# Layer 1 of a four-layer trunk: rotary scores from split operands, and the second rotary queries moved ahead of the heads

## Chip, cores and metric

The kernel runs on one core of one Trainium2 chip. The metric is the device time of one execution in microseconds, given as the median of several runs. A profiled execution of the same program gives the trace: what each engine (PE = TensorE, with PEld for its weight loads; ACT = ScalarE; DVE = VectorE; POOL = GpSimd; SP = SyncE, which issues the loads) did at which microsecond of its span.

## What is computed

The trunk has two layers here (DEPTH = 2): block-sparse attention and a gated MLP, then multi-head latent attention and a second gated MLP, on 256 tokens of width 2048. The change touches only the latent attention of layer 1. Cut to what matters:

```python
def mla_attention(h, pos, wq_a, g_qa, wq_b, wkv_a, g_kva, wkv_b, g_qn, g_kn, g_qr, g_kr, wo):
    cq = rms_norm(h @ wq_a, g_qa)                          # 256 x 512
    q = (cq @ wq_b).reshape(B, S, H, NOPE + RD)            # 16 heads, 128 + 64
    q_nope = rms_norm(q[..., :NOPE], g_qn)
    q_rope = rope(rms_norm(q[..., NOPE:], g_qr), pos, RD)  # 64 rotary features a head
    kv_a = h @ wkv_a                                       # 256 x (512 + 64)
    ckv = rms_norm(kv_a[..., :MLA_KV_RANK], g_kva)
    k_rope = rope(rms_norm(kv_a[..., MLA_KV_RANK:], g_kr)[:, :, None, :], pos, RD)[:, :, 0]
    kv = (ckv @ wkv_b).reshape(B, S, H, NOPE + VD)
    k_nope = rms_norm(kv[..., :NOPE], g_kn)
    v = kv[..., NOPE:]
    ...
        s = (jnp.einsum('bqhd,bkhd->bhqk', qn, k_nope)
             + jnp.einsum('bqhr,bkr->bhqk', qr, k_rope)).astype(F32) * scale
```

The last term is the rotary score: every head has 64 rotary query features of its own, and all heads share one rotary key of 64 features.

## The kernel before, in words

**Weights and split products.** All weight matrices are streamed from HBM in the order of their use, as 370 units of up to 1 MB (L138 to L155), each cut into 2 to 4 pieces of 128 rows by 512 or 288 columns. `Stream.split` (L92) makes of each piece a high part on ACT (L104) and a low remainder on DVE (L105), both in type fp32r. A product of two split operands is three products: high times high, low times high, high times low. With tokens as output rows (`tok_major`, L227) one piece is six products of 512 (or 288) columns at L235; with features as output rows (`feat_major`, L251) it is twelve products of 256 columns at L261 to L263. Operands that are not split are plain f32; for those one product in the program is two products in the trace. The score products (L473, L476) and the value products (L520, L521) are of this kind.

**The order of work** is written out by hand. Every piece is a quantum; `add` (L222) appends it, and `at(q, f)` (L216) hangs a piece of side work behind quantum q. The loop at L984 walks the quanta: first `ws.split` (L987), which has split all pieces up to the third one behind the current one, then the products, then the side work in the order in which it was hung. Each engine executes its own instructions strictly in this order, so a side step that waits on ACT or DVE also holds the splits that stand behind it on that engine, and PE has three further pieces whose parts are ready.

**Layer 1 attention** (L753 to L971) runs in this order of quanta: the query latents (L869); the first half of the rotary queries, heads 0 to 7, four pieces (`rotary_queries(0, 2)`, L920); the key latents and rotary key, 2 x 16 pieces of 288 columns (L922); group 0 of four heads, with queries, keys and values in four pieces each (L948); then the second half of the rotary queries, heads 8 to 15 (L950); groups 1 to 3; then the output projection. The side work that matters:

- `rotary_queries` (L895): evacuation to `qr`, squares (L379), `hr` by a power on POOL (L392), scaling on ACT (L413), rotation on DVE (L435 to L440), and 28 and 29 quanta behind its last piece the two pairs of turns (L449): four 128 x 128 transposes into a PSUM tile `tp` (a pool of two), then one ACT copy (L457) to `qrT`. `qrT` holds two heads in one slot, 64 partitions each.
- The key side: `kva_stats` (L774), with `kvr` on POOL; `kva_scale` (L793); `kva_rotate` (L799), which writes the rotary key twice side by side; `kva_turn` (L813), four transposes of the latents with their evacuation to `ckvT` (L821, L822); `kr_turn` (L826). The last two make two f32 tiles `kr[0]` and `kr[1]` in `room`: POOL writes zeros to all 128 rows (L833), and DVE copies the key to the upper or lower 64 (L834). A head's rotary score multiplies a slot of two heads with the tile that is zero on the other head's rows.
- `Head.plan` (L530): scores and mask, exponentials, normalisation, three transposes (L509), the copy `pT` (L514), values (L520), and the parts of the output (L527, L528).

`DVE` also makes the squares of every query and key head, so it is shared by splits, norms, rotations and softmax.

Of the kernel before, what the change touches and what calls it, by code (L numbers as in the profile page):

```python
# [10 lines left out]
F32 = mybir.dt.float32  # L11
# [6 lines left out]
P = 128  # L18
# [97 lines left out]
def trunk(ctx: ExitStack, tc: tile.TileContext, a, out):  # L116
# [29 lines left out]
    units += grouped("mla_wqr", 1, 0)  # L146
    units += units_of("mla_wkv_a", KVN)
    for g in range(4):
        if g == 1:
            units += grouped("mla_wqr", 1, 1)  # L150
        for name in ("mla_wkn", "mla_wqn", "mla_wv") if g else ("mla_wqn", "mla_wkn", "mla_wv"):
            units += grouped(name, 1, g)
# [200 lines left out]
    class Heads:  # L353
# [63 lines left out]
        def rotate(self, t, stages=(0, 1)):  # L417
# [11 lines left out]
            def part(name):  # L429
                r = att_pool.tile([P, 16 * 32], F32, name=name, bufs=2)  # L430
                return r[:, : n * rot].rearrange("p (n r) -> p n r", n=n)
# [31 lines left out]
    class Head:  # L463
# [4 lines left out]
        def scores(self):  # L468
            sc = ps_sc.tile([P, 512], F32, name="sc")
            qT, kT, i = self.qT(), self.kT(), self.i  # L470
            for q0, n, c in ((0, P, 0), (P, S, P)):
                o = sc[:, c : c + n]
                mm(o, qT[:, i, q0 : q0 + P], kT[:, i, :n], start=True, stop=self.rope is None)  # L473
                if self.rope is not None:
                    qr, kr = self.rope()
                    mm(o, qr[:, q0 : q0 + P], kr[:, :n], start=False, stop=True)  # L476
            self.sc = sc
# [34 lines left out]
        def turned(self):  # L512
            self.pT = att_pool.tile([P, 3 * P], F32, name="pT", bufs=2)
            nc.scalar.copy(self.pT, self.tp[:, : 3 * P])  # L514
# [241 lines left out]
    def open_mla():  # L756
# [6 lines left out]
        env["oT"] = att_pool.tile([P, H, 2 * S], F32R, name="oT", bufs=1)  # L763
        env["qrT"] = att_pool.tile([P, 8, S], F32, name="qrT", bufs=1)

# [8 lines left out]
    def kva_stats():  # L774
        ss = small.tile([P, NT, 2], F32, name="kvss")
        for t in range(NT):
            for k, (lo, hi) in enumerate(((0, 512), (512, 576))):
                junk = att_pool.tile([P, 512], F32, name="kvjunk", tag="ro1", bufs=2)
                nc.vector.tensor_tensor_reduce(
                    out=junk[:, : hi - lo], in0=env["ckv"][:, t, lo:hi], in1=env["ckv"][:, t, lo:hi],  # L780
                    scale=1.0 / (hi - lo), scalar=0.0, op0=ALU.mult, op1=ALU.add,
                    accum_out=ss[:, t, k : k + 1],
                )
# [42 lines left out]
    def kr_turn():  # L826
        tp = ps_tp.tile([P, 512], F32, name="tp")
        for t in range(NT):
            nc.tensor.transpose(
                tp[:, t * P : (t + 1) * P], env["krr"][:, t].rearrange("p i d -> p (i d)"), ident  # L830
            )
        for i in range(2):
            nc.gpsimd.memset(env["kr"][i], 0.0)  # L833
            nc.vector.tensor_copy(env["kr"][i][i * 64 : (i + 1) * 64, :], tp[i * 64 : (i + 1) * 64, :S])  # L834

# [57 lines left out]
    at(q_start + 20, gained_tables)  # L893

    def rotary_queries(u, step):  # L895
        state = {}
# [17 lines left out]
        for i0 in (0, 2):  # L914
            pair = {}
            at(q + step * 14 + i0 // 2, lambda p=pair, i0=i0: hs.turned(None, p, i0))
            at(q + step * 14 + i0 // 2, lambda p=pair, i0=i0: hs.turned_out(
                env["qrT"][:, 4 * u : 4 * u + 4], p, i0))

# [8 lines left out]
    def open_room():  # L928
        t = keep.tile([P, KD * 2 * S + 64], F32, name="room", tag="h")
        env["room"] = t[:, : 32 * S].rearrange("p (k s) -> p k s", k=32)  # L930
        env["kr"] = [env["room"][:, 28 + i] for i in range(2)]

# [4 lines left out]
    for r in range(4):  # L937
        at(q + 3 + r // 2, kva_turn, r)
    at(q + 9, kr_turn)

# [7 lines left out]
    for g in range(4):  # L948
        if g == 1:
            rotary_queries(1, 2)  # L950
        for kind in "kqv" if g else "qkv":
# [12 lines left out]
        for i in range(4):  # L964
            hd = Head(
                4 * g + i, lambda g=g: env["qT", g], lambda g=g: env["kT", g], lambda g=g: env["v", g],
                i, lambda: env["oT"], MLA_SCALE,
                rope=lambda h=4 * g + i: (env["qrT"][:, h // 2, :], env["kr"][h % 2]),
            )
# [133 lines left out]
```

## Time and profile before

| | |
|---|---|
| median of 3 runs | 2100.27 us (2099.58 to 2100.78) |
| profiled execution, its own time | 2100.51 us |
| its span, first to last instruction | 2098.7 us |
| mean granted TensorE clock | 1.000 |
| busy: PE / PEld / DVE / ACT / POOL | 2090.2 / 2014.8 / 1389.4 / 1134.2 / 45.6 us |
| rotary score products (L476) | 64 in the trace, 1199.8 to 1307.5 us |
| rotary queries, first turn (L449) and first wait behind the key latents | 1163.13 us, 1172.18 us |

A row of the timeline gives start, duration, engine, line, operation, output and inputs, partitions and columns, and the count of merged instructions; in brackets stands the idle time ahead of it and what ended it. Products overlap: a 512-column product shows a duration of 0.39 us while the next starts 0.23 us behind it. The pace, start to start, is what a product costs in a stream; the duration is what somebody waits who needs its result. Idle times in brackets count from the modelled end of the last product, so the loss against the pace is larger by the overlap. On ACT and DVE the next instruction likewise starts about 0.1 us ahead of the end of the last.

### The profile page before, as it was taken

What the parts mean: (1) busy time and instruction counts of PE and PEld (TensorE: products, weight loads), DVE (VectorE), ACT (ScalarE), POOL (GpSimd) and SP (SyncE); (2) the same over time, 40 slices, a digit from 0 to 9 for tenths busy, and PEclk for the clock granted to TensorE, in tenths of its full rate; (3) what the DMA queues carried; (4) which work ended last, traced back from release to release, by engine and by line L of the source; (5) the groups of instructions that cost most, each with busy time, mean ns of one, the idle gap of its engine ahead of it and who ended that gap; (6) DMA issues with size and microseconds to landing.
All of it is one profiled execution on the core that took longest, in us unless ns stands there. A gap on an engine that the chain in (4) does not pass through costs nothing.

```text
span 2098.7 us, 42064 instructions
## 1 busy us (share of the span) xinstructions
PE 2090.2 (100%) x16684; PEld 2014.8 (96%) x16684; DVE 1389.4 (66%) x3036; ACT 1134.2 (54%) x2206; POOL 45.6 (2%) x37
## 2 busy tenths in 40 slices
PE   9999999999999999999999999999999999999999
PEld 7888889999999999999999889999999999999999
DVE  6776666766666766655556786767766667655554
ACT  6555555655555555545455675655555555544443
POOL 0000000000000000000000110000000000000000
PEclk9999999999999999999999999999999999999999
DMA  7444445555555555555554533545555555555553
GB/s 272 161 166 176 168 170 188 190 191 201 190 193 201 187 196 199 192 195 195 195 192 158 176 139 106 196 181 200 186 197 198 187 199 195 189 205 208 194 206 131
DMA packets 59381, 391.81 MB, mean 187 GB/s; under 512 B 6960, under 2 KB 10032, under 8 KB 13232
## 3 DMA queue, kind: packets, MB, share of 16 engines
q1 hardware_dynamic: 59040, 388.87, 52.3%
q8 instruction: 130, 2.13, 0.4%
q14 instruction: 67, 0.55, 0.1%
q10 hardware_dynamic: 144, 0.26, 0.1%
HBM read 387.01 MB, written 2.10 MB: 185 GB/s over the span
## 4 chain that ended last, share of the span: by engine, by line
PE 97%; DVE 1%; DMA 1%; issue 0%; ACT 0%; POOL 0%; SPq 0%; ACTq 0%; POOLq 0%
PE acc L261 26%; PE acc L263 26%; PE acc L262 26%; PE acc L235 15%; PE sc L473 1%; PE tp L449 1%; DMA raw<-in_moba_wq 1%; PE sc L520 1%; PE tp L509 0%; PE sc L476 0%; PE sc L521 0%; DVE wlo L105 0%; DMA xT<-in_xT 0%; DVE junk L379 0%; POOL hr L392 0%
## 5 line engine op out<-in xcount | busy, mean ns | idle before, releaser
L105 DVE TENSOR_TENSOR wlo<-raw,whi 128x512 fp32r<-128x512 f32 (+1 forms) x1480 | 1000.5, 684 | 424.6 <-ACT whi L104 422.5
L104 ACT CAST whi<-raw 128x512 fp32r<-128x512 f32 (+1 forms) x1479 | 871.8, 614 | 461.4 <-PE acc L262 213.6
L261 PE MATMUL acc<-h,whi 128*128 128x256 f32 x2880 | 795.3, 276 | 0.0
L263 PE MATMUL acc<-h,wlo 128*128 128x256 f32 x2880 | 794.9, 276 | 0.0
L262 PE MATMUL acc<-h,whi 128*128 128x256 f32 x2880 | 794.9, 276 | 0.0
L262 PEld LDWEIGHTS acc<-h,whi 128*128 128x128 f32 x2880 | 540.7, 188 | 0.0
L261 PEld LDWEIGHTS acc<-h,whi 128*128 128x128 f32 x2880 | 540.6, 188 | 0.0
L263 PEld LDWEIGHTS acc<-h,wlo 128*128 128x128 f32 x2880 | 540.6, 188 | 0.0
L261 PE MATMUL acc<-a,whi 128*128 128x256 f32 x1408 | 388.6, 276 | 0.0
L262 PE MATMUL acc<-a,whi 128*128 128x256 f32 x1408 | 388.6, 276 | 0.0
L263 PE MATMUL acc<-a,wlo 128*128 128x256 f32 x1408 | 388.6, 276 | 0.0
L235 PE MATMUL acc<-whi,h 128*128 128x512 f32 (+1 forms) x896 | 279.8, 385 | 0.7 <-ACT whi L104 0.5
L261 PEld LDWEIGHTS acc<-a,whi 128*128 128x128 f32 x1408 | 264.3, 188 | 0.0
L262 PEld LDWEIGHTS acc<-a,whi 128*128 128x128 f32 x1408 | 264.3, 188 | 0.0
L263 PEld LDWEIGHTS acc<-a,wlo 128*128 128x128 f32 x1408 | 264.3, 188 | 0.0
L235 PEld LDWEIGHTS acc<-whi,h 128*128 128x128 f32 x896 | 164.7, 188 | 31.5 <-ACT h L279 1.3
L235 PE MATMUL acc<-wlo,h 128*128 128x512 f32 (+1 forms) x448 | 169.3, 378 | 0.3 <-DVE wlo L105 0.2
L261 PE MATMUL acc<-oT,whi 128*128 128x256 f32 x512 | 144.8, 283 | 0.0
L263 PE MATMUL acc<-oT,wlo 128*128 128x256 f32 x512 | 141.7, 277 | 0.0
L262 PE MATMUL acc<-oT,whi 128*128 128x256 f32 x512 | 141.6, 277 | 0.0
L675 DVE TENSOR_TENSOR g<-acc,rstd_b 128x256 f32<-128x256 f32 x88 | 37.5, 426 | 126.0 <-PE acc L263 123.1
L682 ACT ACTIVATE c<-g,par 128x256 f32<-128x256 f32 x88 | 53.1, 603 | 108.1 <-DVE g L675 108.1
(141 smaller groups left out, 1558.0 us busy)
## 6 DMA issues: line engine op xcount, KB each, us to landing
raw<-in_ffn_gu SPq DMA_DIRECT2D x176, 1024.0 KB, 4.8
raw<-in_ffn_down SPq DMA_DIRECT2D x88, 1024.0 KB, 4.8
raw<-in_moba_wk SPq DMA_DIRECT2D x16, 1024.0 KB, 4.8
raw<-in_moba_wv SPq DMA_DIRECT2D x16, 1024.0 KB, 4.8
raw<-in_moba_wo SPq DMA_DIRECT2D x16, 1024.0 KB, 4.8
raw<-in_mla_wo SPq DMA_DIRECT2D x16, 1024.0 KB, 4.8
raw<-in_moba_wq SPq DMA_DIRECT2D x13, 1024.0 KB, 4.8
raw<-in_mla_wkv_a SPq DMA_DIRECT2D x8, 576.0 KB, 3.7
```

The costliest lines, as they stand in the source:

```text
L104: self.nc.scalar.copy(hi[:, :n], w)
L105: self.nc.vector.tensor_tensor(lo[:, :n], w, hi[:, :n].bitcast(F32), op=ALU.subtract)
L235: mm(state["acc"][t][:, :n], src[:, kt, c : c + P], (t_lo if part == 1 else t_hi)[:, :n], start=kt == 0 and part == 0, stop=kt == k_last a ...
L261: mm(o, w_hi, src[:, kt, :S], start=first and k == 0, stop=False, skip_group_check=True)
L262: mm(o, w_hi, src[:, kt, S:], start=False, stop=False, skip_group_check=True)
L263: mm(o, w_lo, src[:, kt, :S], start=False, stop=kt == k_last, skip_group_check=True)
L449: nc.tensor.transpose(tp[:, (i * NT + t) * P : (i * NT + t + 1) * P], flat[:, t, c : c + P], ident)
L473: mm(o, qT[:, i, q0 : q0 + P], kT[:, i, :n], start=True, stop=self.rope is None)
L520: mm(o[:, :S], v[:, 0, vs], self.pT[:, :S], start=True, stop=False)
L675: nc.vector.tensor_tensor(self.g[:, 2:], self.gate["acc"][:, :S], self.norm.rstd_b, op=ALU.mult)
L682: nc.scalar.activation(self.c, self.g[:, 2:], AF.Identity, bias=par[:, cb : cb + 1], scale=self.cw(2))
```

## The change

1. **Rotary scores in parts.** The rotary key is kept once, as a high and a low part: `kr` is [128, 2, 256] in fp32r. `kr_turn` fills both with one ACT copy and one DVE subtraction over 128 rows (the key stands on both halves of the rows), in place of two POOL memsets and two DVE copies. Each head gets a slot of its own in `qrT`: the high part of its rotary queries on 64 rows, the low part on the other 64. One product of such a slot with the key's high part gives high times high plus low times high; a second one with the key's low part gives the rest. So a rotary score is two fp32r products for each of the two query blocks, in place of one f32 product.
2. **`rotary_out`** replaces the ACT copy of each pair of turns. For each half of the rows: an ACT copy of 64 rows x 512 to the slots (high), a DVE subtraction to the tile `qrlo` (low; one buffer), and a DMA on POOL's queue that carries the low part to the other 64 rows of the slots, 128 KB each. There are two pairs in each of the two rotary steps, so 8 copies, 8 subtractions and 8 DMAs in all, for 4 copies before.
3. **Order.** The second rotary step (four pieces, their unit of weights, and all side work) stands directly behind the key latents, ahead of group 0, where before it stood behind group 0. The turns of the key latents move from 3 and 4 to 5 and 6 quanta behind the latents, `kr_turn` from 9 to 10.
4. **Room.** `ro1`, `ro2` and the scratch tile of `kva_stats` have one buffer instead of two; the latent heads' `pT` moves into `room`, still with two buffers.

```diff
@@ -145,9 +145,8 @@
     units += units_of("mla_wq_a")
     units += grouped("mla_wqr", 1, 0)
     units += units_of("mla_wkv_a", KVN)
+    units += grouped("mla_wqr", 1, 1)
     for g in range(4):
-        if g == 1:
-            units += grouped("mla_wqr", 1, 1)
         for name in ("mla_wkn", "mla_wqn", "mla_wv") if g else ("mla_wqn", "mla_wkn", "mla_wv"):
             units += grouped(name, 1, g)
     units += units_of("mla_wo")
@@ -427,7 +426,7 @@
                 return s[:, None, :].to_broadcast([P, n, s.shape[1]])
 
             def part(name):
-                r = att_pool.tile([P, 16 * 32], F32, name=name, bufs=2)
+                r = att_pool.tile([P, 16 * 32], F32, name=name, bufs=1)
                 return r[:, : n * rot].rearrange("p (n r) -> p n r", n=n)
 
             if 0 in stages:
@@ -472,8 +471,10 @@
                 o = sc[:, c : c + n]
                 mm(o, qT[:, i, q0 : q0 + P], kT[:, i, :n], start=True, stop=self.rope is None)
                 if self.rope is not None:
+
                     qr, kr = self.rope()
-                    mm(o, qr[:, q0 : q0 + P], kr[:, :n], start=False, stop=True)
+                    for part in range(2):
+                        mm(o, qr[:, q0 : q0 + P], kr[:, part, :n], start=False, stop=part == 1)
             self.sc = sc
 
         def biased(self):
@@ -510,7 +511,10 @@
             self.tp = tp
 
         def turned(self):
-            self.pT = att_pool.tile([P, 3 * P], F32, name="pT", bufs=2)
+            if self.rope is None:
+                self.pT = att_pool.tile([P, 3 * P], F32, name="pT", bufs=2)
+            else:
+                self.pT = env["pT"][self.h % 2]
             nc.scalar.copy(self.pT, self.tp[:, : 3 * P])
 
         def values(self):
@@ -761,7 +765,8 @@
         env["ckvT"] = att_pool.tile([P, 4, 2 * S], F32R, name="ckvT", bufs=1)
         env["cqT"] = att_pool.tile([P, 4, 2 * S], F32R, name="cqT", bufs=1)
         env["oT"] = att_pool.tile([P, H, 2 * S], F32R, name="oT", bufs=1)
-        env["qrT"] = att_pool.tile([P, 8, S], F32, name="qrT", bufs=1)
+        env["qrT"] = att_pool.tile([P, H, S], F32R, name="qrT", bufs=1)
+        env["kr"] = att_pool.tile([P, 2, S], F32R, name="kr", bufs=1)
 
 
     def kva_evac(state, half):
@@ -775,7 +780,7 @@
         ss = small.tile([P, NT, 2], F32, name="kvss")
         for t in range(NT):
             for k, (lo, hi) in enumerate(((0, 512), (512, 576))):
-                junk = att_pool.tile([P, 512], F32, name="kvjunk", tag="ro1", bufs=2)
+                junk = att_pool.tile([P, 512], F32, name="kvjunk", tag="ro1", bufs=1)
                 nc.vector.tensor_tensor_reduce(
                     out=junk[:, : hi - lo], in0=env["ckv"][:, t, lo:hi], in1=env["ckv"][:, t, lo:hi],
                     scale=1.0 / (hi - lo), scalar=0.0, op0=ALU.mult, op1=ALU.add,
@@ -829,9 +834,9 @@
             nc.tensor.transpose(
                 tp[:, t * P : (t + 1) * P], env["krr"][:, t].rearrange("p i d -> p (i d)"), ident
             )
-        for i in range(2):
-            nc.gpsimd.memset(env["kr"][i], 0.0)
-            nc.vector.tensor_copy(env["kr"][i][i * 64 : (i + 1) * 64, :], tp[i * 64 : (i + 1) * 64, :S])
+        hi, lo = env["kr"][:, 0], env["kr"][:, 1]
+        nc.scalar.copy(hi, tp[:, :S])
+        nc.vector.tensor_tensor(lo, tp[:, :S], hi.bitcast(F32), op=ALU.subtract)
 
 
     cq = {}
@@ -892,6 +897,18 @@
 
     at(q_start + 20, gained_tables)
 
+    def rotary_out(pair, j):
+
+
+        heads = env["qrT"].rearrange("p (j i) s -> p i j s", i=2)[:, :, j : j + 2]
+        tp = pair["tp"].rearrange("p (a s) -> p a s", a=2)
+        low = att_pool.tile([P, 2, S], F32R, name="qrlo", bufs=1)
+        for i in range(2):
+            rows, rest = (slice(k * 64, (k + 1) * 64) for k in (i, 1 - i))
+            nc.scalar.copy(heads[rows, i], tp[rows])
+            nc.vector.tensor_tensor(low[rows], tp[rows], heads[rows, i].bitcast(F32), op=ALU.subtract)
+            nc.gpsimd.dma_start(heads[rest, i], low[rows])
+
     def rotary_queries(u, step):
         state = {}
         for kt in range(4):
@@ -914,8 +931,7 @@
         for i0 in (0, 2):
             pair = {}
             at(q + step * 14 + i0 // 2, lambda p=pair, i0=i0: hs.turned(None, p, i0))
-            at(q + step * 14 + i0 // 2, lambda p=pair, i0=i0: hs.turned_out(
-                env["qrT"][:, 4 * u : 4 * u + 4], p, i0))
+            at(q + step * 14 + i0 // 2, rotary_out, pair, 4 * u + i0)
 
     rotary_queries(0, 2)
 
@@ -928,15 +944,16 @@
     def open_room():
         t = keep.tile([P, KD * 2 * S + 64], F32, name="room", tag="h")
         env["room"] = t[:, : 32 * S].rearrange("p (k s) -> p k s", k=32)
-        env["kr"] = [env["room"][:, 28 + i] for i in range(2)]
+        env["pT"] = [t[:, 28 * S + i * 3 * P : 28 * S + (i + 1) * 3 * P] for i in range(2)]
 
     at(q, open_room)
     at(q, kva_stats)
     at(q + 3, kva_scale)
     at(q + 7, kva_rotate)
     for r in range(4):
-        at(q + 3 + r // 2, kva_turn, r)
-    at(q + 9, kr_turn)
+        at(q + 5 + r // 2, kva_turn, r)
+    at(q + 10, kr_turn)
+    rotary_queries(1, 2)
 
     def mla_tiles(g):
         i = 4 * (g % 2)
@@ -946,8 +963,6 @@
         env["v", g] = env["room"][:, 16 + i : 20 + i].rearrange("p (t c) s -> p t (c s)", t=NT)
 
     for g in range(4):
-        if g == 1:
-            rotary_queries(1, 2)
         for kind in "kqv" if g else "qkv":
             state = {}
             for kt in range(4):
@@ -965,7 +980,7 @@
             hd = Head(
                 4 * g + i, lambda g=g: env["qT", g], lambda g=g: env["kT", g], lambda g=g: env["v", g],
                 i, lambda: env["oT"], MLA_SCALE,
-                rope=lambda h=4 * g + i: (env["qrT"][:, h // 2, :], env["kr"][h % 2]),
+                rope=lambda h=4 * g + i: (env["qrT"][:, h], env["kr"]),
             )
             q0 = q_q + 11 + 3 * i
             hd.plan(q0, q0 + 7)
```

## Prediction

> **What bounds the kernel now.** I read the page first, then the chain of waits, then the timelines of layer 1 engine by engine. The page's line of engines and its chain say what counts:
>
> ```profile
> PE 2090.2 (100%) x16684; PEld 2014.8 (96%) x16684; DVE 1389.4 (66%) x3036; ACT 1134.2 (54%) x2206; POOL 45.6 (2%) x37
> PE 97%; DVE 1%; DMA 1%; issue 0%; ACT 0%; POOL 0%; SPq 0%; ACTq 0%; POOLq 0%
> ```
>
> PE sets the time: a microsecond of PE work removed in layer 1 is a microsecond gained, and one in which PE waits there is lost. DVE and ACT count only where PE runs out of split pieces. The view by stretches shows where that already happens:
>
> ```profile
> 1163.00:1170.00 7.00, 7.00 (x48) 6.51 (x47) 4.29 (x14) 5.41 (x11) 0.09 (x1) 1.00 0.82 304
> 1170.00:1181.00 11.00, 10.04 (x48) 7.96 (x47) 8.86 (x32) 6.45 (x13) 1.30 (x1) 1.00 0.42 144
> 1181.00:1190.00 9.00, 7.86 (x35) 5.59 (x34) 7.73 (x38) 4.10 (x9) 2.45 (x3) 1.00 0.48 174
> 1230.00:1260.00 30.00, 30.00 (x166) 25.75 (x165) 25.62 (x108) 22.40 (x56) 3.89 (x2) 1.00 0.41 141
> ```
>
> (Length, then busy PE, PEld, DVE, ACT, POOL, clock, DMA share, GB/s.) PE has holes behind the key latents, at 1170 to 1190, and none among the heads, though DVE is 85% busy there. The holes in PE's timeline:
>
> ```profile
> 1171.04 0.39 PE L235 MATMUL acc<-whi,cqT 128*128 128x512 f32 x1
> 1172.18 0.30 PE L816 MATMUL tp<-ident,ckv 128*128 128x128 f32 x1 [0.76 <-DVE ckv L793]
> 1172.68 0.55 PE L816 MATMUL tp<-ident,ckv 128*128 128x128 f32 x3 [0.20 <-DVE ckv L793]
> 1173.30 0.39 PE L235 MATMUL acc<-wlo,cqT 128*128 128x512 f32 x1
> ...
> 1181.49 0.39 PE L235 MATMUL acc<-whi,ckvT 128*128 128x512 f32 x1
> 1182.53 0.33 PE L829 MATMUL tp<-ident,krr 128*128 128x128 f32 x1 [0.34 <-DVE krr L811]
> 1182.93 0.40 PE L235 MATMUL acc<-wlo,ckvT 128*128 128x512 f32 x1
> ...
> 1186.83 0.39 PE L235 MATMUL acc<-whi,cqT 128*128 128x512 f32 x1
> 1188.01 0.50 PE L235 MATMUL acc<-wlo,cqT 128*128 128x512 f32 x1 [0.79 <-DVE wlo L105]
> ```
>
> Against the pace (0.23 us for a 512-column product, 0.11 for a transpose) the first hole is larger than its brackets: the product of 1171.04 frees PE at 1171.27, the piece goes on 0.23 ahead of 1173.30, that is 1173.07, and 0.44 of the 1.80 between are four transposes: **1.36**. The second: 1181.72 to 1182.70 less two transposes, **0.76**. The third: 1187.06 to 1188.01, **0.95**. In all 3.1 us.
>
> **Part 1, the products.** A head's scores:
>
> ```profile
> 1199.54 0.38 PE L473 MATMUL sc<-room 128*128 128x128 f32 x2
> 1199.76 0.39 PE L476 MATMUL sc<-room,qrT 128*128 128x128 f32 x2
> 1199.98 0.60 PE L473 MATMUL sc<-room 128*128 128x256 f32 x2
> 1200.42 0.59 PE L476 MATMUL sc<-room,qrT 128*128 128x256 f32 x2
> 1201.08 0.40 PE L235 MATMUL acc<-wlo,ckvT 128*128 128x512 f32 x1
> ...
> 1271.26 0.28 PE L261 MATMUL acc<-oT,whi 128*128 128x256 f32 x1
> 1272.16 0.28 PE L263 MATMUL acc<-oT,wlo 128*128 128x256 f32 x1
> ...
> 1136.51 0.39 PE L235 MATMUL acc<-whi,cqT 128*128 128x512 f32 x1
> 1136.74 0.50 PE L856 MATMUL tp<-ones,cacc 128*128 128x1 f32 x4
> 1137.42 0.40 PE L235 MATMUL acc<-wlo,cqT 128*128 128x512 f32 x1
> ```
>
> An f32 rotary score of 128 keys costs 1199.98 - 1199.76 = 0.22; one of 256 keys 0.43 (1200.42 to 0.23 ahead of 1201.08). An fp32r product of 256 columns costs (1272.16 - 1271.26) / 8 = 0.113, so two cost 0.23 and a head gains 0.20 on its second query block; sixteen heads, **-3.3 us**. The trace has no fp32r product of 128 columns. Bounds: half of 0.113, if columns alone count, which would give another -1.7 us for 32 products; and 0.22, as slow as the f32 score, which would give +3.5. I take 0.11, because it is the least that any pair of weight load and product takes here: the four products of a single column take 1136.74 to 1137.19, 0.11 each, and so do the transposes. At 0.11 two parts cost what the f32 score does, and the first query block gains nothing.
>
> [...]
>
> **Part 2, `rotary_out` behind the first rotary queries.** Nothing of it stands in a stage without cover, but it makes a round trip. In the built program three waits matter: the second ACT copy of a pair waits for the first DVE subtraction; the first subtraction of the next pair waits until both DMAs of this pair have landed, `qrlo` having one buffer; and, being in program order, the splits behind wait on both engines. The rows of before at that place:
>
> ```profile
> 1163.76 0.59 ACT L457 COPY qrT<-tp 128x512 f32<-128x512 f32 x1 [1.58 <-PE tp L449]
> 1164.99 0.59 ACT L457 COPY qrT<-tp 128x512 f32<-128x512 f32 x1 [0.31 <-PE tp L449]
> 1165.47 1.66 ACT L104 CAST whi<-raw 128x512 fp32r<-128x512 f32 x3
> ...
> 1156.19 0.69 DVE L440 TENSOR_TENSOR qr<-ro,ro 128x512 f32<-128x512 f32 x1
> ...
> 1167.16 0.39 PE L235 MATMUL acc<-whi,cqT 128*128 128x512 f32 x1
> ...
> out<-xT SPq DMA_DIRECT2D x16, 128.0 KB, 1.8
> xT<-in_xT SPq DMA_DIRECT2D x4, 128.0 KB, 3.9
> ```
>
> 64 rows take as long as 128 with the same 512 elements a row: 0.59 a copy, 0.69 a subtraction, 0.03 between them. First pair: copy 1163.76 to 1164.35, subtraction to 1165.07, second copy to 1165.69, second subtraction to 1166.41, second DMA issued 1166.44. No row shows a DMA on POOL's queue. Two rows have its size, 128 KB: 1.8 us at the quiet end of the kernel and 3.9 us in its busy start. I take **3.2**, nearer the upper, since the 16 DMA engines are 82% busy in this stretch and POOL must issue as well: landed 1169.64. Only then the second pair: subtraction to 1170.37, second copy 1170.40 to 1170.99, the last subtraction to 1171.71. The next high part runs beside it, up to 1171.51, its low part on DVE to 1172.3. PE has three pieces split ahead when the second pair is turned, and uses them up by 1167.16; it then starts at about 1171.6 and waits another 0.55 for the low part: **5.05 us lost**.
>
> What it takes away: with four rotary pieces (5.5 us) between the latents and their turns, `kva_scale` is done in time and the first hole of 1.36 closes. Place A: +5.05 - 1.36 = **+3.7**.
>
> **Part 3, the order behind the latents.** The second hole (0.76) goes: `kr_turn` has three quanta behind `kva_rotate` instead of two, and PE is late anyway. The third hole changes its cause:
>
> ```profile
> 1146.54 2.98 POOL L392 TENSOR_TENSOR hr<-hms,mhalf 128x16 f32<-128x16 f32 x1 [7.67 <-DVE hms L387]
> 1182.70 1.94 POOL L392 TENSOR_TENSOR hr<-hms,mhalf 128x8 f32<-128x8 f32 x1 [11.40 <-DVE hms L387]
> 1184.59 0.56 POOL L833 MEMSET room<- 128x256 f32 x2
> 1184.93 0.86 DVE L834 COPY room<-tp 64x256 f32<-64x256 f32 x2 [1.18 <-POOL room L833]
> ```
>
> DVE waited 1.18 for POOL's zeros, behind the 1.94 us power of the first query heads; from that came PE's 0.95. Now the zeros are gone, but the rotary step's power over 16 columns (2.98) comes due one quantum ahead of the query heads' (1.94), on a POOL that does them in turn: 4.9 us from the first, while DVE has some 2.5 us of squares and splits to do before it needs the second. It waits about 2.4, 1.2 more than now, and PE's 0.95 becomes 2.15. Place B: 1.2 - 0.76 = **+0.4**. The four DMAs stand before `kvr` on POOL, and are issued before the sums for it exist. On SP one load of 1 MB is moved ahead of three; the loads run three units ahead, and I cost it at nothing. If that lead were gone it would be a landing, some 5 us.
>
> **Part 2 again, among the heads.** The second rotary step's turns now fall among the heads of groups 0 and 1. From the first pair's transposes to the second DMA it is 0.16 + 2.65 us, 3.2 more to its landing, then 2.0 for the second pair's subtraction, copy and subtraction: 8.0. The `tp` pool has two tiles, and the one of the second pair is wanted again by the turns of a head's probabilities (L509). By the built order PE has until then a head's scores (1.1), a piece (1.39), the second turns (0.44), values (0.66), turns (0.44) and a piece (1.39): 5.4. So it stands 2.7 us, and about 0.8 more at the next turns, whose tile waits for an ACT copy that stood behind the same wait. Place C: **+3.6** at 0.41 DMA share, with the same 3.2. The extra 8 subtractions (5.5 us of DVE) have cover in DVE's 15% of free time otherwise; ACT's four additional copies too.
>
> **Costed at nothing:** the one-buffer `ro1`, `ro2` and scratch, since DVE alone writes and reads them in its own order; `pT` in `room`, two buffers as before; the ACT copy and subtraction of `kr`, for two DVE copies of 64 rows, which leave it the time. If DVE had no free time there, a copy is 0.4 us.
>
> **Sum:** -3.3 + 3.7 + 0.4 + 3.6 = **+4.4 us**. From the profiled execution's 2100.51 (its span 2098.7 and 1.8 around it; the median of the three runs is 2100.27) that gives **2104.9 us**. A measurement can tell about 0.2% (4.2 us) from no change.
>
> **Rivals.**
> - *The copies land sooner.* Places A and C each move by as much as the landing does. At 1.8 us the sum is 4.4 - 2.8 = +1.6, 2102.1; at 3.9 it is +5.8. Below about 3.0 us the kernel is not measurably slower. For it: the cores' own SBUF on both sides, and a third of the DMA time used at C. Against: POOL has to issue. [...]
> - *128-column fp32r products cost 0.22:* +3.5, 2108.4. For it: f32 products of that width do. Against: one product in place of two.
> - *They cost 0.06:* -1.7, 2103.2. Against it: nothing in the trace goes below 0.11.
> - *The waits hide* (other side): if ACT and DVE had enough split ahead, A and C would fall out: 4.4 - 5.05 - 3.6 = -4.3, 2096.2, and less with quicker products. It decides at A: the second pair would have to start by 1165.2 for PE to be served at 1167.16, but the second DMA is only issued at 1166.44. It needs a wait that I read in the program not to bind.
> - *The order does not close the old holes:* if `kr_turn` still came too early, 0.76 more, 2105.7; inside the forecast's own chance.
>
> **Chances.** The forecast 0.44, the slow products 0.17 (both slower by over 0.2%): **0.61**. Early copies 0.20, quick products 0.13 and a hundredth of the hidden waits: within 0.2% **0.34**. Hidden waits otherwise: faster by over 0.2% **0.05**. The range takes in the bounds: low 1.8 us and 0.06 together, 2100.51 + 4.4 - 2.8 - 1.7 = 2100.4; high 3.9 and 0.22, 4.4 + 1.4 + 3.5 = 9.3, 2109.8.
>
> **What would show it.** PE idle before a `whi` product near 1171 by some 4 us, ended by ACT, with DVE idle for the DMAs ahead of `qrlo`; no idle before L816; POOL's two powers back to back and a DVE wait above 2 us on the second; PE idle before the turns of a head around 1235 by some 3 us; two fp32r rotary products of 128 columns at 0.11 apart and of 256 at 0.113. I am wrong if the DMAs land in under 2 us or over 4, or if 128 columns cost far from 0.11.

## The result, and the profile after

The changed kernel takes **2111.36 us** (median of 6 runs, 2109.79 to 2112.22), beside 2100.29 us (2099.58 to 2101.51, 6 runs) for the kernel before: a ratio of 1.0049, 95% interval 1.0039 to 1.0059. It is slower by 11.1 us. The prediction had the sign and +4.4 us; its range ended at 2109.8. The profiled execution has a span of 2110.4 us, 11.7 above that of before.

First the same four stretches by the view of windows of the changed kernel (length, busy PE, PEld, DVE, ACT, POOL, granted clock, DMA share, GB/s):

```profile
1163.00:1170.00 7.00, 5.04 (x38) 4.58 (x36) 1.97 (x4) 2.17 (x4) 1.34 (x2) 1.00 0.77 239
1170.00:1181.00 11.00, 5.72 (x13) 4.16 (x14) 6.80 (x17) 4.77 (x9) 2.56 (x3) 0.57 0.35 104
1181.00:1190.00 9.00, 9.00 (x43) 7.41 (x42) 6.03 (x25) 5.71 (x11) 0.00 (x0) 0.95 0.62 221
1230.00:1260.00 30.00, 27.36 (x145) 23.07 (x144) 22.18 (x86) 19.30 (x48) 5.37 (x6) 0.94 0.39 123
```

Read two columns. PE's busy time fell in the first two rows by 1.96 and 4.32 us and in the last by 2.64: PE stands at places A and C. And the granted clock, 1.00 in all four rows of before, is 0.57, 0.95 and 0.94. No term of the sum held that. DVE, which the rival of fuller engines would have at its limit, is less busy than before in the first two rows: it waits.

Place A in PE's timeline, and the engines behind it (DVE, ACT, POOL):

```profile
1168.04 0.29 PE L234 MATMUL acc<-whi,h 128*128 128x288 f32 x1
1175.27 0.80 PE L234 MATMUL acc<-whi,cqT 128*128 128x512 f32 x1 [6.94 <-ACT whi L104]
1176.08 0.80 PE L234 MATMUL acc<-wlo,cqT 128*128 128x512 f32 x1
1176.67 1.06 PE L234 MATMUL acc<-whi,cqT 128*128 128x512 f32 x2
1177.52 0.63 PE L234 MATMUL acc<-wlo,cqT 128*128 128x512 f32 x1
...
1182.29 0.39 PE L234 MATMUL acc<-wlo,cqT 128*128 128x512 f32 x1
```

```profile
1173.28 0.68 DVE L909 TENSOR_TENSOR qrlo<-tp,qrT 64x512 fp32r<-64x512 f32 x1 [5.93 <-DMA qrT<-qrlo]
```

```profile
1173.99 0.58 ACT L908 CAST qrT<-tp 64x512 fp32r<-64x512 f32 x1 [6.80 <-DVE qrlo L909]
1174.60 1.66 ACT L104 CAST whi<-raw 128x512 fp32r<-128x512 f32 x3
```

```profile
1165.83 0.76 POOL L910 DMA_DIRECT2D qrT<-qrlo  x1 [15.86 <-DVE qrlo L909]
1167.17 0.58 POOL L910 DMA_DIRECT2D qrT<-qrlo  x1 [0.58 <-DVE qrlo L909]
```

This is the chain that was foretold, link by link: copies issued, DVE waits for their landing ahead of the second pair's first subtraction, ACT waits for that subtraction, ACT's next high part (1174.60) waits behind, and PE waits for the high part. Only its length differs. PE stands 7.10 us ahead of 1175.27, another 0.58 ahead of 1176.08 and 0.45 earlier (at 1167.41), 8.1 in all instead of 5.05. After it the 512-column products run 0.43 us apart (1177.52 less 1176.67, for two) where 0.23 is the pace. The four transposes of the latents have no idle time ahead of them any more.

The two landings, each from the view of DMAs over a stretch that holds one issue of POOL (median us from issue to landing last); beside the second stands the weight load that SP issues at 1167.38:

```profile
qrT<-qrlo POOLq DMA_DIRECT2D x1, 128.0 KB, 3.5
```

```profile
raw<-in_mla_wkn SPq DMA_DIRECT2D x1, 1024.0 KB, 5.6
qrT<-qrlo POOLq DMA_DIRECT2D x1, 128.0 KB, 6.0
```

Issued at 1167.17, the second copy landed 6.0 us later, at 1173.2; the 1 MB load that SP issued 0.2 us behind it landed at 1167.38 + 5.6 = 1173.0. The first copy, too, landed just behind a load: at 1165.83 + 3.5 = 1169.3, that of 1161.95 at 1169.0.

The load does not stand 0.2 us behind the second copy by chance. SP waits for a low-part split of DVE before it issues the load (`SPq L71 <- DVE wlo L105` in the view of waits, 5.0 us at the longest), and that split stands directly behind the pair's two subtractions, whose end also releases the copy:

```profile
1166.89 0.46 DVE L105 TENSOR_TENSOR wlo<-raw,whi 128x288 fp32r<-128x288 f32 x1
```

```profile
1167.38 0.33 SPq L71 DMA_DIRECT2D raw<-in_mla_wkn  x1
```

Products and place C, in PE's timeline:

```profile
1215.16 0.38 PE L472 MATMUL sc<-room 128*128 128x128 f32 x2
1215.30 0.42 PE L477 MATMUL sc<-kr,qrT 128*128 128x128 f32 x2
1215.55 0.65 PE L472 MATMUL sc<-room 128*128 128x256 f32 x2
1215.85 0.59 PE L477 MATMUL sc<-kr,qrT 128*128 128x256 f32 x2
1216.28 0.39 PE L234 MATMUL acc<-whi,cqT 128*128 128x512 f32 x1
...
1238.71 0.39 PE L234 MATMUL acc<-whi,cqT 128*128 128x512 f32 x1
1241.22 0.52 PE L510 MATMUL tp<-ident,s 128*128 128x128 f32 x3 [2.13 <-DVE qrlo L909]
1242.26 0.66 PE L448 MATMUL tp<-ident,qk 128*128 128x128 f32 x4 [0.52 <-ACT room L459]
```

A head's scores take 1216.28 - 1215.16 = 1.12 us, against 1201.08 - 0.23 - 1199.54 = 1.31 before: 0.19 a head. The saving is not divided as forecast: a head's first query block takes 1215.55 - 1215.16 = 0.39 where it took 0.44, the second 0.73 where it took 0.87. What a 128-column product costs by itself is not to be had from these rows, since the f32 products beside it moved as well (0.14 and 0.30 from start to start, before 0.22 and 0.44). At C PE stands 1241.22 - 1238.71 - 0.23 = 2.28 and then 0.68.

Place B, in POOL's and PE's timelines:

```profile
1196.75 4.62 POOL L391 TENSOR_TENSOR hr<-hms,mhalf 128x16 f32<-128x16 f32 x2 [15.83 <-DVE hms L386]
1203.61 0.50 PE L234 MATMUL acc<-wlo,ckvT 128*128 128x512 f32 x1 [1.07 <-DVE wlo L105]
```

The two powers run back to back, DVE waits 2.07 us for the second (at 1201.41), and PE waits for DVE.

**Account.** Place A 8.1 - 1.36 = +6.8; halved clock behind A: 15 products take 1182.29 - 1176.08 = 6.2 us instead of 15 x 0.23 = 3.5, +2.7; place B -0.2 (gaps of 0.31, 1.23 and 0.2 against 1.9 before); place C +3.0; halved clock behind C +1.6 (worked out in the same way over 1243.2 to 1246.9); products 16 x 0.19 = -3.0. Sum +10.9. Of the 11.7 between the spans 0.5 lie ahead of this stage (its first product starts at 1134.44 instead of 1133.99), and 0.3 I don't assign.

### The profile page after: what moved, and what is told of

Same layout as the page of the kernel before. It is cut to its first block, busy times and chain, and to the rows that moved or that the text cites. A ratio compares the mean times of both kernels' runs of the same rounds, so it can differ in the third digit from the quotient of the medians.

```text
span 2110.4 us, 42091 instructions
## 1 busy us (share of the span) xinstructions
PE 2092.2 (99%) x16684; PEld 2016.2 (96%) x16684; DVE 1394.5 (66%) x3043; ACT 1137.2 (54%) x2211; POOL 50.0 (2%) x43
## 4 chain that ended last, share of the span: by engine, by line
PE 97%; DVE 1%; DMA 1%; ACT 0%; issue 0%; POOL 0%; SPq 0%; DVEq 0%; POOLq 0%; ACTq 0%
PE acc L261 26%; PE acc L262 26%; PE acc L260 26%; PE acc L234 16%; PE sc L472 1%; PE tp L448 1%; PE sc L524 1%; PE tp L510 0%; DMA qrT<-qrlo 0%; DVE wlo L105 0%; DVE junk L378 0%; PE sc L525 0%; PE sc L477 0%; DMA xT<-in_xT 0%; POOL hr L391 0%
## 5 line engine op out<-in xcount | busy, mean ns | idle before, releaser
L105 DVE TENSOR_TENSOR wlo<-raw,whi 128x512 fp32r<-128x512 f32 (+1 forms) x1480 | 1000.9, 684 | 419.4 <-ACT whi L104 417.1
```

The lines of the kernel that those rows point to most:

```text
L105: self.nc.vector.tensor_tensor(lo[:, :n], w, hi[:, :n].bitcast(F32), op=ALU.subtract)
```

## Experiments

All were timed beside the kernel before, whose medians were 2100.56 to 2100.94 in these comparisons.

| kernel | median us | ratio to before, 95% interval | PE stands at A, C (us) |
|---|---|---|---|
| changed kernel | 2111.36 | 1.0049 (1.0039 to 1.0059) | 8.1, 3.0 |
| two buffers of `qrlo` | 2100.78 | 1.0001 (0.9992 to 1.0010) | 2.2, 1.8 |
| copies first | 2107.37 | 1.0033 (1.0021 to 1.0045) | 7.3, 1.4 |
| both | 2098.45 | 0.9989 (0.9980 to 0.9998) | 1.6, 0.5 |
| filler in A | 2108.53 | 1.0037 (1.0025 to 1.0050) | 2.0 beside 6 of filler, 3.0 |
| copies on SP's queue | 2106.35 | 1.0026 (1.0016 to 1.0037) | 4.8, 2.8 |
| copies on ACT's queue | 2111.93 | 1.0056 (1.0043 to 1.0068) | 6.9, 5.6 |
| load held back | 2107.37 | 1.0031 (1.0020 to 1.0042) | 4.5, 3.0 |
| order alone | 2099.44 | 0.9994 (0.9985 to 1.0002) | 0, 0 |
| scores alone | 2110.38 | 1.0045 (1.0032 to 1.0057) | 8.1, 3.1 |
| both, and an earlier power | 2096.63 | 0.9981 (0.9972 to 0.9990) | 1.6, 0.5 |

### Two buffers of `qrlo`: is it the landing, or the added work?

```diff
-        low = att_pool.tile([P, 2, S], F32R, name="qrlo", bufs=1)
+        low = att_pool.tile([P, 2, S], F32R, name="qrlo", bufs=2)
```

(`krr` shares a buffer with `ro2`, and `cacc` one with `qrlo`, to make room.)

> The changed kernel with two buffers of qrlo instead of one (room for the second is made by letting two scratch tiles share a buffer). Nothing of the computation is changed. Theory (landing): the second pair's first subtraction stands behind the landing of the first pair's two DMAs, because qrlo has one buffer; from that come PE's 8.1 us of stalls at 1167 to 1176, the 3.0 us at 1241, and the halved clock behind each. With two buffers no pair of a step waits for the other's DMAs: no PE gap above 1 us at either place, granted clock 1.00 from 1160 to 1260, and a time near that of the kernel before, -0.4 us from it by my working (products -3.3, the rest from fuller DVE and ACT), 2097 to 2102. Rival (load): the eight more subtractions and four more copies overfill DVE and ACT, and the landing lies beside that; then the buffer brings at most 2 us and the time stays at 2109 or more.

2100.78 us: 10.6 us less than the changed kernel, with every added copy, subtraction, DMA and product still in it. The landing theory holds and the load theory falls. PE's timeline at A:

```profile
1167.16 0.29 PE L234 MATMUL acc<-whi,h 128*128 128x288 f32 x1
1168.50 0.50 PE L234 MATMUL acc<-whi,cqT 128*128 128x512 f32 x1 [1.04 <-ACT whi L104]
1169.30 0.50 PE L234 MATMUL acc<-wlo,cqT 128*128 128x512 f32 x1 [0.31 <-DVE wlo L105]
1169.64 0.63 PE L234 MATMUL acc<-whi,cqT 128*128 128x512 f32 x2
1170.11 0.40 PE L234 MATMUL acc<-wlo,cqT 128*128 128x512 f32 x1
```

One gap of 1.2 us where there were 7.10, and the pace is 0.23 right behind it; the granted clock is 1.00 throughout. The copies land no sooner than before (the second takes 6.8 us here); nobody waits for them. My bound of 1 us a gap was missed by 0.2 at A and 0.1 at C.

### Copies first: which engine's wait?

```diff
+        for i in range(2):
+            rows = slice(i * 64, (i + 1) * 64)
+            nc.scalar.copy(heads[rows, i], tp[rows])
         for i in range(2):
             rows, rest = (slice(k * 64, (k + 1) * 64) for k in (i, 1 - i))
-            nc.scalar.copy(heads[rows, i], tp[rows])
             nc.vector.tensor_tensor(low[rows], tp[rows], heads[rows, i].bitcast(F32), op=ALU.subtract)
```

> The changed kernel with both ACT copies of a pair ahead of both subtractions; qrlo keeps its one buffer. Nothing of the computation is changed. Theory (landing): ACT no longer waits for DVE, so high parts go on, but DVE still waits some 6 us for the DMAs and the low parts behind it with it; PE's stall at the first place gets shorter by 1 to 3 us and keeps most of its length, the clock still halves behind it; 3 us less than the changed kernel, 2107 to 2110. Rival (load): the wait of ACT on DVE is what counts, not the landing; then the stall goes nearly whole and the time falls to 2102 or less.

2107.37 us, as the landing theory has it. The timeline of PE shows that only the name of the wait changed at A:

```profile
1175.02 0.79 PE L234 MATMUL acc<-wlo,cqT 128*128 128x512 f32 x1 [6.74 <-DVE wlo L105]
```

ACT goes on and splits its high part; PE now waits for DVE's low part, which stands behind the same landing. The stalls got shorter by 0.8 us at A, where I had expected 1 to 3, and by 1.6 at C, behind which the clock no longer halves. Neither edit alone breaks both links of the chain; the two together, below, do.

### A filler in the stall: does the stall halve the clock?

```diff
+    def filler():
+        t = ps_sc.tile([P, 512], F32, name="sc")
+        for _ in range(28):
+            mm(t, zeros[:, :P], zeros, start=True, stop=True)
+
+    at(len(quanta) - 1 + 32, filler)
```

> The changed kernel with 28 additional bf16 products of zeros, 512 columns each, placed behind the last piece of the latents, into a score tile that nobody reads, so that PE is busy for some 6 us of its 7.1 us stall at the first place. Their result is used nowhere and the computation is unchanged. Theory (a stall halves the clock): the stall's end stays where it is, since it is DVE's and ACT's, but PE is not seen idle, so the granted clock stays 1.00 there and the fp32r products behind run 0.23 us apart instead of 0.43; about 3.3 us less than the changed kernel, 2107 to 2109. Rival (the clock halves for another reason, such as the burst of work, or the trace's clock says nothing of the pace): products still 0.43 apart from 1175 to 1182 and the time the same as the changed kernel's or some us more, 2111 to 2115.

2108.53 us, 2.8 less than the changed kernel, for 6 us of additional work on the engine that sets the time. In PE's timeline the 28 products fill 1167.8 to 1173.8 (27 are recorded):

```profile
1167.82 5.99 PE L941 MATMUL sc<-zeros 128*128 128x512 bf16 x27
1174.65 0.50 PE L234 MATMUL acc<-whi,cqT 128*128 128x512 f32 x1 [0.84 <-ACT whi L104]
1175.46 0.50 PE L234 MATMUL acc<-wlo,cqT 128*128 128x512 f32 x1 [0.32 <-DVE wlo L105]
1175.80 0.64 PE L234 MATMUL acc<-whi,cqT 128*128 128x512 f32 x2
1176.28 0.40 PE L234 MATMUL acc<-wlo,cqT 128*128 128x512 f32 x1
```

The stall ends just where it did (1174.65 - 1167.46 = 7.2 us behind the start of the last latent product, as in the changed kernel), the pace behind it is 0.23, and the clock stays at 1.00 until C (in the two windows of 1168.39 to 1175.22 PE is busy for 3.41 and 2.51 us, where the changed kernel has 0.14 and 0.00). So the halved clock at A came of PE's idleness, and its price there, 2.7 in the account, is 2.8 by the two medians and 3.1 by their differences from the kernel before.

### Copies on SP's and on ACT's queue, and the load held back: why 6 us?

```diff
-            nc.gpsimd.dma_start(heads[rest, i], low[rows])
+            nc.sync.dma_start(heads[rest, i].bitcast(F32), low[rows].bitcast(F32))
```

> The changed kernel with the DMAs of the low parts issued on SP's queue instead of POOL's, nothing else changed. Theory A (POOL's issue is what is slow: its DMAs start late while DVE and POOL are both at work): on SP the same 128 KB lands in 2 to 2.5 us at the first place as well, PE's stall there falls from 7.1 to about 3 us, and the time by 4 to 7 us with less of the halved clock, 2104 to 2107. Theory B (the 16 DMA engines are busy with weights there, 0.8 of the time, and the copy stands behind those): it lands in 4 to 6 us all the same, 2109 to 2112, or later if SP's loads queue behind its wait for DVE.

2106.35 us, theory A's number. But the edit does two things: SP issues in order, so its next load, `mla_wkn`, also stands behind all four copies (1172.10 instead of 1167.38). The first pair lands in 4.0 and 2.9 us, at 1169.0 and 1169.2, just behind the load that SP had issued at 1161.37 (7.3 us, landed at 1168.7); the second pair lands in 2.3 and 2.4. The gap that was 7.10 us is 3.77, not 3. So this run alone can't say whether POOL's queue or the load was the cause. The next two take them apart. First `nc.scalar.dma_start` in the same line:

> The changed kernel with the four copies of a rotary step issued on ACT's queue instead of POOL's; SP's order of weight loads is as in the changed kernel, so the 1 MB load of mla_wkn still starts 0.2 us behind the second copy. Nothing of the computation is changed. Theory A (the copy shares the DMA engines with that load): the second copy still lands in 5 to 6 us, PE stands some 7 us at the first place with the halved clock behind it, 2109 to 2113. Theory B (POOL's issue or queue is slow): it lands in 2.3 to 4 us as it did on SP's queue, and the time falls to 2104 to 2107.

2111.93 us lies in theory A's range, for another reason: ACT now waits for each subtraction ahead of each issue (up to 2.15 us at a time), so its high parts are late by themselves, and SP's load started 1.6 us behind the second copy, not 0.2; that copy landed in 2.4. So it doesn't answer the question as I put it. It tells something else: the copy that ACT issues at 1170.58, inside the load of 1168.98 to 1174.0, takes 3.9 and lands at 1174.5 (one issued between 1237.6 and 1237.7 takes 5.5). So on ACT's queue, too, a copy landed behind the load that it met, by 0.5 us. Then the load held back, POOL's queue kept:

```diff
             nc.gpsimd.dma_start(heads[rest, i], low[rows])
+        if j == 0:
+            held = small.tile([P, 16], F32, name="held")
+            nc.sync.dma_start(held[:64], heads[:64, 1, 0, :16].bitcast(F32))
```

> The changed kernel with one small SP DMA added (64 rows of 16 numbers of the copied low parts, into a tile that nobody reads) behind the first pair's copies, so that SP's next weight load, mla_wkn, starts only when the copies have landed; the copies stay on POOL's queue. The output's computation is unchanged. Theory A (shared with the load): the second copy lands in 2.3 to 4 us although it is on POOL's queue, PE's stall at the first place falls from 7.1 to 4 to 5.5 us, and the time by 2 to 5 us, 2106 to 2109, unless the load that is held becomes late itself. Theory B (POOL's queue): the copy takes 6 us still, and the time is 2111 or more.

2107.37 us, theory A. The view of DMAs for the issues at 1166.91, 1169.92 and 1170.34 of this kernel, one after the other:

```profile
qrT<-qrlo POOLq DMA_DIRECT2D x1, 128.0 KB, 2.3
```

```profile
raw<-in_mla_wkn SPq DMA_DIRECT2D x1, 1024.0 KB, 5.9
qrT<-qrlo POOLq DMA_DIRECT2D x1, 128.0 KB, 6.0
```

With no load behind it the second copy lands in 2.3 us on POOL's queue; the third, issued 0.4 us behind the load, takes 6.0. Queue and size are the same: the load decides. In the changed kernel, too, every copy outside a load landed in 2.3, and those at A and C that met one landed 0.2 to 1 us behind it. PE's stall at A falls to 3.44 + 0.58 + 0.45 = 4.5; the gap that was 7.10 is 3.44, less than the 4 to 5.5 I had expected.

The copies of the changed kernel one by one, in the view of DMAs: 3.5, 6.0, 2.3 and 2.3 us at A, 2.3, 2.3, 3.4 and 2.6 at C. The four of 2.3 had no load in flight at their issue; the other four met a load. With two buffers the second copy had a load issued 0.2 us behind it (1166.50), took 6.8 and landed 0.2 behind that load. A load issued later didn't delay the copy: 0.7 us behind the last of the four at A on SP's queue (that pair took 2.3 and 2.4), 1.3 behind the copy of 1236.67 on POOL's queue in the changed kernel (2.3).

### Order alone and scores alone: which half of the change?

Order alone is the kernel before with `grouped("mla_wqr", 1, 1)` and `rotary_queries(1, 2)` behind the latents, `kva_turn` at 5 and `kr_turn` at 10. Scores alone is the changed kernel with those four put back.

> The kernel before with the order of the change alone: second rotary queries directly behind the latent keys, the turns of the latents and of the rotary key later; the scores stay f32 with 128 rows, without DMAs and subtractions. Nothing of the computation is changed. By the prediction's own steps: holes one and two (1.36 and 0.76 us) close, place B adds 1.2: 0.9 us less than before, 2099 to 2100.5, and no halved clock. Rival (the order itself is what crowds DVE and ACT): PE stands 3 us or more in 1160 to 1190 and the time is 2103 or more.

2099.44 us, at the number of the steps (0.9 less than before; measured 1.5 less, whose interval just reaches no change). The holes ahead of the latents' and the rotary key's turns are gone, and only place B is left, 0.68 and 1.11 us of waits for `wlo`.

> The changed kernel's scores, copies, subtractions and DMAs in the order of the kernel before: second rotary queries behind the first group's tiles, turns of the latents as before. Nothing of the computation is changed. Theory (the round trip costs what it costs in either order): the first rotary step's second pair waits for landings of about 6 us as in the changed kernel, PE stands 6 to 7 us at the first place with the halved clock behind it, the three old holes stay or come near it, and the second step's round trip costs 3 to 4 us among the heads: 2110 to 2115, not below the changed kernel. Rival (only the moved order makes the copies late): landings of 2.5 us, and 2105 or less.

2110.38 us, as expected, with a stall of 7.04 us at A ended by ACT's high part, the same 6 us landing (`mla_wv` starts 0.2 us behind the copy there), and two halved stretches (products 0.43 us apart at 1178.44 and at 1270.03). So the loss belongs to the copies, not to the order.

### Both edits, and a version that beats both kernels

Two buffers and copies first:

> Two buffers of qrlo and both ACT copies ahead of both subtractions; nothing of the computation is changed. With two buffers alone the kernel measured 2100.78, and PE still stood 2.2 us at the first place (ended by ACT's high part, which waits for DVE's first subtraction) and 1.8 us among the heads. Theory (what is left is ACT waiting for DVE inside a pair): both fall to 1 us or less in sum, and the time is 2 to 3 us below two buffers alone, 2097.5 to 2099. Rival (what is left is the extra work on a full DVE): the stalls move to the low parts and the time stays within 1 us of 2100.8.

2098.45 us, 2.3 less than two buffers alone, as the theory has it: most of what was left was ACT's wait inside a pair. The stalls fell from 4.0 to 2.1 us in sum, not to 1 or less; the largest that stays at A, 1.2 us, is now ended by DVE's low part, as the rival has it. Then the second rotary step's squares and power earlier:

```diff
-            at(q + step * (1 + t), hs.squares, t)
-        at(q + step * 3, hs.rstd)
+            at(q + ((1, 3)[t] if u else step * (1 + t)), hs.squares, t)
+        at(q + (4 if u else step * 3), hs.rstd)
```

> Two buffers of qrlo, both copies first, and of the second rotary step the squares and the power one to two pieces of the order earlier, so that POOL has done its 2.98 us power before the query heads' power of 1.94 us comes due; nothing of the computation is changed. Theory: the stalls of 0.3 and 1.3 us at place B close as well, about 1.5 to 2 us less than with two buffers and copies first, 2095.5 to 2097.5, faster than the kernel before by some 0.2%. Rival: DVE is full there, so the earlier squares push a split and the gain is under 0.5 us.

2096.63 us, a ratio of 0.9981 (0.9972 to 0.9990): 4.3 us less than the kernel before, whose median was 2100.94 in this comparison. What changed at place B is seen in POOL's timeline of this kernel:

```profile
1183.50 3.21 POOL L391 TENSOR_TENSOR hr<-hms,mhalf 128x16 f32<-128x16 f32 x1 [10.34 <-DVE hms L386]
1187.44 1.95 POOL L391 TENSOR_TENSOR hr<-hms,mhalf 128x8 f32<-128x8 f32 x1 [0.73 <-DVE hms L386]
```

POOL is idle for 0.73 us between the powers instead of doing them back to back, and PE has no idle time left at place B.

## Why the prediction was wrong, point by point

- **The bound: right.** PE set the time in every kernel here, and closed gaps came back as time: two buffers close 7.1 us of stalls and 4.3 of halved clock, and the time falls by 10.6.
- **Part 1, products: right in the sum of a head**, 0.19 measured and 0.20 forecast, but not in its parts: the first query block gains 0.05 where 0 was forecast, the second 0.14 where 0.20 was. That two 128-column fp32r products cost what one f32 product did is not shown by itself. Both rivals on their price fall by the sum, which would have been no gain or 0.31 a head.
- **Part 2, the round trip at A: the chain right, its size wrong; this is the first of two steps that failed.** The prediction took 3.2 us for the landing, "nearer the upper" of two SP rows, as though a copy's time grew with the share of busy engines. What was measured is not a share: 2.3 us where no load held the copy up, and else a landing 0.2 to 1 us behind that load. The deciding copy took 6.0; the prediction's own sign of being wrong, a landing over 4, came true. That is +2.8 on the term, and POOL issued the copy 0.3 us behind the end of its subtraction: together the +3.1 by which the stall exceeds 5.05. The 64 rows did take as long as 128: 0.58 a copy and 0.68 a subtraction. The trace of before showed the loads at this place, in SP's timeline:

```profile
1161.49 0.33 SPq L71 DMA_DIRECT2D raw<-in_mla_wkn  x1
1165.20 0.33 SPq L71 DMA_DIRECT2D raw<-in_mla_wv  x1
1170.46 0.33 SPq L71 DMA_DIRECT2D raw<-in_mla_wqr  x1
```

  The loads start 3.7 and 5.3 us apart, and that of 1165.20 took 4.8 us to land; a copy issued at 1166.4 could hardly miss them. That the copy lands only behind the load it meets, no row of before shows. Nor did the prediction ask what its subtractions do to the loads: the split ahead of the load of 1165.20 is the one that now stands behind them, and the load came 0.2 us behind the copy.
- **A halved clock: not in the sum at all; this is the second step that failed.** The prediction forecast a stall of 5.05 us and put nothing for the clock behind it, without a reason. It cost 2.7 behind A and 1.6 behind C. The filler shows the cause and the first price. With the load held back PE stands only 4.5 us at A, and the granted clock is 0.50 from 1171.0 to 1177.8 all the same (the products of 1171.35 and 1172.16 show 0.79 us each, in the changed kernel 0.80, with two buffers 0.50): the term was missing at the forecast's own stall too. Together with the landing this is 4.3 + 2.8 = 7.1 us, against a miss of 11.1 - 4.4 = 6.7.
- **Part 3, place B: the mechanism right, its balance off by 0.6.** The powers run back to back and PE waits for `wlo`, 1.7 us in all against 1.9 before; forecast +0.4, measured -0.2. Order alone confirms the closed holes.
- **Part 2 among the heads, place C: right in stalls**, 3.0 against 3.6, with the first copies landing in 2.3 where 3.2 was taken (no load in flight at their issue), and the halved clock on top.
- **The rivals.** *Copies land sooner* is half true where no load is in flight (2.3 us, between its 1.8 and the 3.2 taken), and false where it counts (6.0). *The waits hide* fell in the changed kernel; two buffers make it come true in part (4.0 us of stalls stay), and the time then is that of before.
- **What holds the copy up stays open, but its data itself came late.** In the view of DMAs a copy has 144 packets on POOL's queue. Up to 1169.0 us of the changed kernel 144 have started, those of the first copy, which landed at 1169.3; from 1169.0 to 1170.2 none; and the 144 of the second between 1170.2 and 1173.0, beside the last 93 of the load. So the second copy's data itself started at least 3.0 us behind the issue, where the copy of 1174.26 started 1.1 us behind its own. What made it late, no run here tells.

## What to carry to other kernels

A wait for an on-chip copy of 128 KB cost 2.3 us here, and 2.6 to 6.0 in the changed kernel where it met a weight load: the copy then landed 0.2 to 1 us behind that load. Before adding such a copy, look at the timeline of the load queue at the time of the issue, ask what your own steps do to the release of the next load, and give the copy's source a second buffer so that nobody waits for its landing. Price a long stall of the tensor engine with the halved clock behind it: here 2.7 us behind A and 1.6 behind C, after windows of 3.41 us with 0.14 and 1.54 us busy (next section). When two engines hand work to each other inside a pair of steps, issue all of one engine's part first.

## What the runs showed of the hardware that was not expected

In the changed kernel the granted clock changes on a grid of 3.41 us: it falls at 1171.60, comes back at 1181.84 (3 steps), falls at 1243.28 (18 steps) and comes back at 1246.70 (one). That kernel on this grid, at A and at C, in the view of windows (PEclk is the third number from the end):

```profile
1164.78:1168.19 3.41, 3.13 (x24) 2.80 (x22) 1.83 (x3) 1.62 (x4) 1.34 (x2) 1.00 0.64 211
1168.19:1171.60 3.41, 0.14 (x2) 0.00 (x0) 0.00 (x0) 0.00 (x0) 0.00 (x0) 1.00 0.96 298
1171.60:1175.02 3.42, 0.00 (x0) 0.00 (x0) 1.10 (x2) 1.00 (x2) 0.58 (x1) 0.50 0.17 51
1175.02:1178.43 3.41, 3.15 (x7) 2.17 (x8) 3.20 (x9) 3.15 (x7) 0.58 (x1) 0.50 0.44 77
1178.43:1181.84 3.41, 3.41 (x10) 2.65 (x9) 3.34 (x11) 1.24 (x2) 1.41 (x1) 0.50 0.26 41
1181.84:1185.26 3.42, 3.42 (x16) 2.80 (x15) 1.18 (x3) 1.61 (x3) 0.00 (x0) 1.00 0.64 268
```

```profile
1236.46:1239.87 3.41, 2.64 (x16) 1.99 (x14) 2.13 (x7) 1.36 (x4) 0.58 (x1) 1.00 0.69 115
1239.87:1243.28 3.41, 1.54 (x10) 1.25 (x11) 2.50 (x11) 3.38 (x10) 1.16 (x2) 1.00 0.98 340
1243.28:1246.70 3.42, 3.42 (x12) 2.87 (x11) 2.23 (x13) 1.43 (x3) 0.00 (x0) 0.50 0.04 6
```

It halved at the end of windows with 0.14 and 1.54 us busy and came back at the end of full ones (3.41 and 3.42), so both stalls were paid for after them; 3.15 of 3.41 us busy did not yet bring it back at A, the full window behind it did. The window ahead of the drop at C isn't wholly idle: PE is busy 1.54 of 3.41 us. The copies on SP's queue had nearly the same stall at C (2.11 and 0.68 us), 1.70 us busy in its window, and no drop (1.00 from 1239.15 to 1242.57, too):

```profile
1235.74:1239.15 3.41, 1.70 (x10) 1.38 (x11) 2.65 (x12) 3.39 (x10) 0.00 (x0) 1.00 0.64 120
```

The filler kernel dropped at C with 1.63 busy (0.50 from 1240.07), the kernel with the load held back with 1.51 (0.50 from 1239.28); two buffers, with 1.8 us of stalls at C, did not (1.00 from 1230 to 1260). In these runs, then, the border at C lies between 1.63 and 1.70 us busy, near half a window, by records whose ends are modelled; nearly the same stall crossed it in the changed kernel and not with the copies on SP's queue. The stall at C, 2.28 us and 0.68 behind it, of which 1.35 and 0.68 fell inside one window, cost a whole window at half clock, 1243.28 to 1246.70.
